# Nine products on ones at the start, a last store in two halves, and twelve of the 44 weight sums made by DMA moved from attention into gate and up

## The chip, the cores and the metric

One core of a Trainium2 chip runs the whole program; the other cores do nothing. The metric is the time of one execution in device microseconds (us). The kernel before took 2303.65 us in the median of three runs (2301.34 to 2307.2). Lower is better. All durations, waits and start times below come from one further execution, the profiled one.

## The reference, cut to what matters

One decoder block on 512 tokens with model width 2048 and a feed-forward width of 5632, everything in fp32:

```python
h = rms_norm(x, g_mix)
# one projection h @ w_in, split into NSA queries/keys/values, gates, and GLA queries/keys/values
x = x + concat(rms_norm(o_nsa), o_gla) @ w_out
hq, hm = rms_norm(x, g_cross), rms_norm(mem, g_mem)         # 256 memory tokens
ck = rms_norm((hm @ w_ck).reshape(B, M, 4, 128), g_ck)       # the "key projection" below
x = x + softmax(cq @ ck.T) @ (hm @ w_cv) @ w_co
hf = rms_norm(x, g_ffn)
gg, uu = split(hf @ w_gu)                                    # gate and up
return x + (silu(gg) * uu) @ w_down                          # down
```

## The kernel before, in words

**Products.** A product of two fp32 operands is made of three products of split operands. `split` (L155 to L160) has ACT cast a tile to its rounded part (`wh`, `qh`, `X`) and DVE subtract to get the rest (`wl`, `ql`); `mm3` then has PE multiply high by high, low by high and high by low. Nearly every product has a 128x128 stationary part and 512 columns. PE is recorded at L98, ACT and DVE mostly at L158 to L160. In the names, `X` is the split input x, `wh`/`wl` a split weight of attention, mixing or cross attention, `qh`/`ql` a split weight of gate, up or down, `PA`/`PB` and `hT`, `ss`, `C`, `T` work tiles, `mm`, `t`, `s`, `o` the pairs of PSUM banks.

**Stages.** The first projection reads x row by row (`load_x`, L334: load, split, square for the norm) and its weights `w_v` (natural order, 0 to about 60 us). Attention (NSA and GLA together) runs to about 640 us, with small pieces of work from generators interleaved by a counter of ticks (`Flows`, L100). Mixing (`w_out`) runs to about 785 us, then the key projection (`project_keys`: four `w_ck` tiles of 2048 columns, each loaded in two pieces of 512 KB by SP at L188 through a pool of two raw tiles named `w`), then the rest of cross attention to about 1010 us. Gate and up take 1010 to 1871 us in eleven blocks n = 0 to 10, each of a phase 1 (loads of 768 KB, L1264, 24 products for each of 8 steps kp) and a phase 2 (loads of 512 KB, L1275, 18 products for each kp). Down runs from 1871 us to the end.

**Sums of weights.** The products of down and of gate and up are made by a scheme with fewer products that needs sums of blocks of weights. Those of `w_down` are made by DMA alone, DRAM to DRAM: a copy of 512 KB from `w_down` into a tile `td` (L145), and a second transfer that adds another block to it (L143, an accumulating transfer). There are 44 such sums for `td`, 88 transfers, and 8 more for tiles `tw` (L1405 and L1409). All of these transfers are issued by POOL, one after the other in its queue, with whatever else POOL issues (spills of attention, loads of `mem_t`, `w_cq`, x1 and h).

**What sets their places.** `SUMS` (L47) is a table of (first tick, last tick, number of sums); the 88 transfers of `td` become marks of `flows`. When a mark is recorded, the copy or the accumulation is issued with a dependency on the PE product recorded last (`last_mm`), so it cannot leave before PE has come there. With this table, 16 sums lie at 92 to 270 us, 4 at 321 to 380, 14 at 440 to 622, and 10 at 690 to 835, that is beside mixing and the key projection. Each `tw` pair (copy and accumulation together) hangs on kp 5 of phase 2 of n = 1 to 8. The dictionary `extra` that `phase` takes names what is to be called after which kp.

**The start.** POOL sets `ones`; ACT casts it to `ones_r` in two halves (L224). The square of every x row is made by ACT directly behind that row's cast (L341), and DVE adds it to `ss` (L343).

**The end.** `gather` (L1584) adds the last product bank to the residual `PA` on DVE and calls `store` (L1579), which issues a 256 KB transfer on SP (L1582).

Of the kernel before, what the change touches and what calls it, by code (L numbers as in the profile page):

```python
# [13 lines left out]
AF = mybir.ActivationFunctionType  # L14
OP = mybir.AluOpType
# [11 lines left out]
AHEAD = 150  # L27
# [16 lines left out]

LAG = 3

SUMS = ((80, 190, 16), (222, 268, 4), (298, 388, 14), (440, 546, 10))  # L47

SV = {}
_n = 0  # L50
# [9 lines left out]
def hybrid_block(ctx: ExitStack, tc: tile.TileContext, x_t, mem_t, sv, cmat, umask, w_a, w_r67, w_v, w_vg, w_v3,  # L60
                 w_vsw, w_gk2, w_c1, w_c2, w_out, w_cq, w_ck, w_cv, w_co, w_gu, w_down, y_t):
    nc = tc.nc
# [24 lines left out]
    def bank(tag):  # L87
        return psp.tile([128, 512], F32, name=tag, tag=tag, bufs={"mm": 3, "s": 2, "t": 2, "o": 1}[tag])
# [3 lines left out]
    def row(tag, dt=F32):  # L92
        return sb([128, 512], tag, BUFS[tag], dt)
# [3 lines left out]
    def mm(*args, **kw):  # L97
        last_mm[0] = PE.matmul(*args, **kw)  # L98
# [56 lines left out]
    def split(hi, lo, src, gain=None):  # L155

        if gain is None:
            return S.copy(hi, src), V.tensor_sub(lo, src, hi)  # L158
        return (S.activation(hi, src, AF.Copy, scale=gain),
                V.scalar_tensor_tensor(lo, src, gain, hi, op0=OP.mult, op1=OP.subtract))  # L160

    def split_row(src, gain=None, tag="X"):
        pair = row(tag, F32R), row(tag, F32R)
        split(*pair, src, gain)
        return pair

    class Weights:
# [53 lines left out]
    ones = pool.tile([128, 64], F32, name="ones")  # L221
    G.memset(ones, 1.0)
    for a in (0, 64):
        S.copy(ones_r[:, a:a + 64], ones)  # L224

    gains = held_vecs[:, NSV:NSV + 2]
    V.tensor_scalar(gains[:, 0:1], vec("g_q"), -HEAD_SCALE, None, op0=OP.mult)
# [103 lines left out]
    xg = []  # L331
    ss = row("ss")

    def load_x(kt):  # L334
        xr = row("st")
        with tc.high_priority(offset=0 if kt < 4 else 40 if kt < 8 else 100):
            nc.sync.dma_start(xr, x_t[:, kt, :])
        xg.append(split_row(xr, vec("g_mix", kt)))
        sq = ss if kt == 0 else row("n")
        with tc.high_priority(offset=200 if kt == KT - 1 else -20 if kt < 4 else 0):  # L340
            S.activation(sq, xr, AF.Square)  # L341
            if kt:
                V.tensor_add(ss, ss, sq)  # L343

    def x_ahead(kq):
        while kq and len(xg) < min(4 * kq + 4, KT):
# [532 lines left out]
    ss = row("ss")  # L879
# [382 lines left out]
    def weights_1(n, kp):  # L1262
        raw = sb1("raw")
        nc.sync.dma_start(raw[:, :1536], w_gu[n, kp, :, 512:2048])  # L1264
        V.tensor_sub(raw[:, 0:1024], raw[:, 0:1024], raw[:, 512:1536])  # L1265
        a = split_cols(raw, 0, 1024)
        V.tensor_add(raw[:, 1536:2048], raw[:, 0:512], raw[:, 1024:1536])
        kept[kp] = sb1("T2")
        S.copy(kept[kp], raw[:, 1536:2048])
        b = split_cols(raw, 1024, 1024)  # L1270
        return part(b, 512, 512), part(b, 0, 512), part(a, 0, 512), part(a, 512, 512)
# [127 lines left out]

    tw = {(step, kp): dram.tile([128, 1024], F32, name="tw", tag="tw", bufs=8) for kp in range(4) for step in (1, 3)}  # L1400

    def make_sum(step, kp):
        def go():
            a, b = (w_down[0, kp], w_down[1, kp]) if step == 1 else (w_down[2, kp], td[kp][:, 1024:])
            i = G.dma_start(tw[step, kp], a)  # L1405
            tc.add_manual_dep(i.ins, last_mm[0].ins.name,
                              mybir.DependencyInfo(mybir.DependencyClass.Sync, mybir.DependencyReason.DATA),
                              reason="in its turn")
            G.dma_start(tw[step, kp], b, accum_op=OP.add, max_dma_last_dim=2048)  # L1409
        return go  # L1410

    ready_made = [make_sum(*k) for k in tw]
    rc2 = []
    gate = []
    hs = None
# [1 line left out]
    for n in range(NB):  # L1417
        if n == 0:
            b1, bp = first_banks
            u, c11 = [sb2("C") for _ in range(2)], [sb2("C") for _ in range(2)]  # L1420
            with tc.high_priority(offset=2 * EVICT):
                for i in range(2):
                    fa = S.copy(u[i], b1[i])
                for i in range(2):
                    fv = V.tensor_add(c11[i], u[i], bp[i])
            bu, b2, b3 = [bank("mm"), bank("mm")], [bank("mm"), bank("o")], [bank("t"), bank("t")]

            def last_sums():
                with tc.high_priority(offset=AHEAD):
                    for kp in (KP - 2, KP - 1):  # L1430
                        with tc.issue_after(splits_b[kp - KP + 3][0].ins), tc.issue_after(splits_b[kp - KP + 3][1].ins):
                            form_sums(kp)

            phase(lambda kp: weights_b(n, kp), (bu, b2, b3), (4, 5, 3), (1, 2, 0), (0, 1, 2), True, 40,
                  {2: [last_sums]}, (fa, fv))
        else:
            b1 = c11 = [bank("mm"), bank("mm")]
            bu = [bank("s"), bank("s")]
            b2 = [bank("t"), bank("t")]
            b3 = [bank("mm"), bank("o")]  # L1440
            phase(lambda kp: weights_1(n, kp), (bu, b1, b2, b3), PHASE_1, (2, 3, 1, 0), (1, 0, 2, 3), True, AHEAD, {},
                  fence)
            u = [sb2("C") for _ in range(2)]
        c22 = [sb2("C") for _ in range(2)]
        with tc.high_priority(offset=EVICT):
            for i in range(2):
                if n:
                    fa = S.copy(u[i], b1[i])
                V.tensor_add(u[i], u[i], bu[i])
            for i in range(2):  # L1450
                V.tensor_add(c22[i], u[i], b2[i])
            for i in range(2):
                fv = V.tensor_add(c22[i], c22[i], b3[i])
        extra = {}
        if hs:
            extra = {2: [turn(hs, n - 1, 0)], 4: [turn(hs, n - 1, 1)], 6: [lambda: gate.append(last_mm[0])]}
            if ready_made:
                extra[5] = [ready_made.pop(0)]
        if n == 0:
            def scales():  # L1460
                ss2 = sb2("C")
                G.dma_start(ss2, ssd)
                rc2.append(token_norm_col(ss, D, NT, ss2))

            phase(lambda kp: weights_c(n, kp), (b2, b3), (2, 6), (0, 1), (0, 1), False, AHEAD, {3: [scales]}, (fv,))
            rc2 = rc2[0]
        else:
            phase(lambda kp: weights_2(n, kp), (b1, b2, b3), PHASE_2, (1, 0, 2), (0, 1, 2), False, AHEAD, extra,
                  (fa, fv))
        g1, g2 = [sb2("C") for _ in range(2)], [sb2("C") for _ in range(2)]  # L1470
        with tc.high_priority(offset=EVICT):
            for i in range(2):
                fa = S.activation(g1[i], c11[i], AF.Silu, scale=rc2[:, i:i + 1])
            for i in range(2):
                V.tensor_add(g2[i], u[i], b2[i])
            for i in range(2):
                fv = V.tensor_add(u[i], u[i], b3[i])
        fence = fa, fv
        for i in range(2):
            S.activation(g2[i], g2[i], AF.Silu, scale=rc2[:, 2 + i:3 + i])  # L1480
        for i in range(2):
            V.scalar_tensor_tensor(g1[i], u[i], rc2[:, i:i + 1], g1[i], op0=OP.mult, op1=OP.mult)
        for i in range(2):
            V.scalar_tensor_tensor(g2[i], c22[i], rc2[:, 2 + i:3 + i], g2[i], op0=OP.mult, op1=OP.mult)
        hs = g1 + g2
# [95 lines left out]
        c = 1024 * b + 512 * j  # L1581
        nc.sync.dma_start(y_t[2 * a + i, :, c:c + 512], res[a, b][x])  # L1582

    def gather(op, a, b, src, x, last=False):  # L1584
        op(res[a, b][x], res[a, b][x], src[x])
        if last:
            store(x, a, b)
# [12 lines left out]
    for step, plan in enumerate(STEPS):  # L1600
# [9 lines left out]
        for kp in range(NK):  # L1610
            if step or kp % 2 == 0:
                load_w(step, kp)
                late_splits(step, kp)

            if kp in (1, NK - 1):
                for r in rs_ if kp == 1 or step == 2 else reversed(rs_):
                    for x in range(4):
                        for k in (kp - 1, kp):
                            down_product(step, r, k, (x,))
                        if step == 3 and kp == NK - 1:  # L1620
                            gather(ADD, *((0, 0), (1, 0))[r], banks[r], x, True)
            elif 1 < kp < NK - 2:
                for r in rs_:
                    down_product(step, r, kp, range(4))
            if step == 0 and kp % 2 and 5 <= kp < 21:
                for m in (kp - 5, kp - 4):
                    if m % 4 == 0:
                        raw = sb1("raw")
                        nc.sync.dma_start(raw, x2d[m // 4])
                    turn_x2(m, raw)  # L1630
            if step == 0 and kp in (2, 4):
                turn(hs, NB - 1, kp // 2 - 1, "t")()
            if step == 0 and kp in (5, 11):
                load_h(0, len(GRP) - (2 if kp == 5 else 1))
            if step < 3 and kp % 4 == 3:
                load_h(step + 1, kp // 4)
# [138 lines left out]
```

## Time and profile before

| what | value |
|---|---|
| median of three runs | 2303.65 us (2301.34 to 2307.2) |
| the profiled execution's own time | 2308.06 us |
| its span, first to last instruction | 2306.3 us |
| mean granted TensorE clock | 0.997 |
| PE busy | 2284.3 us (99%) |
| DVE, ACT, POOL busy | 1662.3 (72%), 1181.8 (51%), 164.0 us (7%) |
| products and transposes on PE | 10764 records |

The profiled execution lies 4.4 us above the median of the runs, and 1.76 us of its own time lie outside the span. Engines are PE (matmul), DVE (vector), ACT (scalar), POOL and SP (here, issuers of transfers). A row of the timeline gives start, duration, engine, line, operation, written tile, read tiles; in brackets stands how long the engine had been idle before it and what it was released by. In rows of the chain of waits stand start, duration, and engine or transfer. The chain of waits leads back from the last instruction, at each step to what released it.

### The profile page before, as it was taken

To read this page: it belongs to the slowest core of one execution; us is meant where nothing else is said; L and a number is where in the kernel's file an instruction comes from. 1 tells how busy PE (TensorE), PEld (TensorE's weight loads), DVE (VectorE), ACT (ScalarE), POOL (GpSimd) and SP (SyncE) were. 2 spreads that over 40 slices of the span, in tenths; PEclk is the share of its full clock that TensorE was granted. 3 is DMA by queue.
4 is the path that set the end of the run, shared out by engine and by line. 5 is a ranking of instruction groups with operands and counts; after the bars stand their busy time and mean duration, and the time that the engine had idled before them with its cause. 6 is when DMAs were issued, how large, how long until landed. Compare 5 with 4: busy or idle time off the path is not lost.

```text
span 2306.3 us, 29509 instructions
## 1 busy us (share of the span) xinstructions
PE 2284.3 (99%) x10764; PEld 1895.6 (82%) x10764; DVE 1662.3 (72%) x2552; ACT 1181.8 (51%) x1857; POOL 164.0 (7%) x240
## 2 busy tenths in 40 slices
PE   8999999999999999999999999999999999999999
PEld 7988888888878878777888888888888888888887
DVE  6478766677775446688888788888887875775685
ACT  6334545556774335665555545544554555444452
POOL 0011100011111100110000000000000000000000
PEclk9999999999999999999999999999999999999999
DMA  6587656466658754685456545644564497766754
GB/s 191 135 195 180 172 155 172 123 174 174 167 170 236 205 161 141 205 219 179 148 180 196 161 140 183 200 155 156 187 189 149 141 333 292 269 230 245 267 207 146
DMA packets 140449, 434.17 MB, mean 188 GB/s; under 512 B 14448, under 2 KB 34928, under 8 KB 136848
## 3 DMA queue, kind: packets, MB, share of 16 engines
q1 hardware_dynamic: 80752, 306.96, 39.5%
q0 software_dynamic: 33824, 96.75, 17.6%
q10 hardware_dynamic: 25728, 28.58, 3.5%
q8 instruction: 84, 1.38, 0.2%
q14 instruction: 61, 0.50, 0.1%
HBM read 390.81 MB, written 94.11 MB: 210 GB/s over the span
## 4 chain that ended last, share of the span: by engine, by line
PE 92%; DVE 3%; DMA 3%; issue 1%; ACT 1%; SPq 0%; ACTq 0%; DVEq 0%
PE mm L98 50%; PE t L98 16%; PE s L98 14%; PE o L98 10%; DVE ql L158 1%; PE t L800 1%; PE s L1361 1%; DVE wl L158 1%; DMA w<-w_ck 1%; DMA raw<-w_down 0%; DMA raw<-w_gu 0%; DMA w<-w_c 0%; ACT wh L158 0%; PE t L1575 0%; DVE PB L158 0%
## 5 line engine op out<-in xcount | busy, mean ns | idle before, releaser
L158 ACT CAST qh<-raw 128x1024 fp32r<-128x1024 f32 (+1 forms) x526 | 510.1, 980 | 480.0 <-PE t L98 126.8
L158 DVE TENSOR_TENSOR ql<-raw,qh 128x1024 fp32r<-128x1024 f32 (+1 forms) x526 | 590.2, 1130 | 149.9 <-PE mm L98 53.2
L98 PE MATMUL mm<-X,wh 128*128 128x512 f32 x1600 | 504.6, 395 | 0.0
L98 PEld LDWEIGHTS mm<-X,wh 128*128 128x128 f32 x1600 | 294.5, 188 | 56.6 <-issue 0.8
L98 PE MATMUL t<-qh,PB 128*128 128x512 f32 x968 | 335.4, 391 | 0.0
L98 PE MATMUL mm<-X,wl 128*128 128x512 f32 x800 | 313.9, 393 | 0.3 <-DVE wl L158 0.3
L98 PE MATMUL mm<-qh,PB 128*128 128x512 f32 x868 | 310.7, 391 | 1.7 <-ACT qh L158 1.7
L158 DVE TENSOR_TENSOR wl<-w,wh 128x1024 fp32r<-128x1024 f32 (+2 forms) x150 | 179.4, 1199 | 163.9 <-ACT wh L158 161.9
L158 ACT CAST wh<-w 128x1024 fp32r<-128x1024 f32 (+2 forms) x150 | 154.2, 1030 | 246.1 <-PE mm L98 169.5
L98 PE MATMUL s<-qh,PB 128*128 128x512 f32 x672 | 232.9, 391 | 0.1
L98 PE MATMUL mm<-qh,PA 128*128 128x512 f32 x640 | 221.7, 389 | 0.0
L98 PEld LDWEIGHTS t<-qh,PB 128*128 128x128 f32 x968 | 181.9, 188 | 37.3
L98 PEld LDWEIGHTS mm<-qh,PB 128*128 128x128 f32 x868 | 163.1, 188 | 36.7 <-ACT qh L158 2.9
L98 PE MATMUL t<-ql,PB 128*128 128x512 f32 x484 | 188.3, 389 | 0.0
L98 PE MATMUL o<-qh,PB 128*128 128x512 f32 x484 | 187.6, 390 | 0.0
L98 PEld LDWEIGHTS mm<-X,wl 128*128 128x128 f32 x800 | 150.4, 188 | 32.8 <-DVE wl L158 1.6
L98 PE MATMUL mm<-ql,PB 128*128 128x512 f32 x434 | 169.8, 391 | 2.1 <-DVE ql L158 2.1
L98 PEld LDWEIGHTS s<-qh,PB 128*128 128x128 f32 x672 | 125.9, 188 | 26.5 <-ACT qh L158 1.0
L98 PEld LDWEIGHTS mm<-qh,PA 128*128 128x128 f32 x640 | 120.1, 188 | 25.3
L98 PE MATMUL s<-ql,PB 128*128 128x512 f32 x336 | 131.5, 391 | 0.2
L98 PE MATMUL mm<-ql,PA 128*128 128x512 f32 x320 | 124.5, 389 | 0.0
L1265 DVE TENSOR_TENSOR raw<-raw 128x1024 f32<-128x1024 f32 x80 | 97.3, 1217 | 31.9 <-DMA raw<-w_gu 31.9
(498 smaller groups left out, 3449.0 us busy)
## 6 DMA issues: line engine op xcount, KB each, us to landing
raw<-w_gu SPq DMA_DIRECT2D x88, 768.0 KB, 4.3
raw<-w_gu SPq DMA_DIRECT2D x88, 512.0 KB, 3.5
raw<-w_down SPq DMA_DIRECT2D x84, 512.0 KB, 4.7
td<-w_down POOLq DMA_DIRECT2D x66, 512.0 KB, 6.6
w<-w_a SPq DMA_DIRECT2D x60, 512.0 KB, 4.5
raw<-td SPq DMA_DIRECT2D x22, 1024.0 KB, 4.9
PB<-h POOLq DMA_DIRECT2D x35, 512.0 KB, 5.7
h<-T ACTq DMA_DIRECT2D x66, 256.0 KB, 4.2
```

The costliest lines, as they stand in the source:

```text
L98: last_mm[0] = PE.matmul(*args, **kw)
L158: return S.copy(hi, src), V.tensor_sub(lo, src, hi)
L800: PE.transpose(tp[:, 128 * (i - j):128 * (i - j) + 128], ps_[b][:, POFF[i] + 128 * j:POFF[i] + 128 * j + 128], ident)
L1265: V.tensor_sub(raw[:, 0:1024], raw[:, 0:1024], raw[:, 512:1536])
L1361: PE.transpose(ps[f][:, 128 * i:128 * i + 128], hs[i][:, c:c + 128], ident)
```

## The change

It makes four edits.

1. Nine products of `ones_r` with itself go into a `t` bank at the very start; nobody reads the bank. `ones_r` is cast by DVE instead of ACT.
2. The square of x row 0 (`ss`) is issued only behind the cast of x row 1.
3. The last store is halved: the last tile of down is added in two parts of 256 columns, the first stored by SP, the second by ACT's queue.
4. `SUMS` keeps 2 sums at ticks 298 to 311 and 10 at 323 to 388 where it had 14 at 298 to 388, and the 10 at ticks 440 to 546 are gone. The remaining 12 sums (24 transfers, `LATE_SUMS`) join the 16 transfers of `tw` in one list of 40; `two_sums` takes two from its head for each of the 20 phases of n = 1 to 10, one after kp 3 and one after kp 7. Copy and accumulation are thus issued apart, each with its own dependency on the last product.

```diff
-SUMS = ((80, 190, 16), (222, 268, 4), (298, 388, 14), (440, 546, 10))
+SUMS = ((80, 190, 16), (222, 268, 4), (298, 311, 2), (323, 388, 10))
+LATE_SUMS = 12
...
-        split(*pair, src, gain)
+        last_cast[0] = split(*pair, src, gain)[0]
...
-        S.copy(ones_r[:, a:a + 64], ones)
+        V.tensor_copy(ones_r[:, a:a + 64], ones)
+    idle = bank("t")
+    for i in range(9):
+        mm(idle.rearrange("p (a n) -> p a n", a=4), ones_r, ones_r[:, None, :].to_broadcast([128, 4, 128]),
+           start=True, stop=True)
...
         xg.append(split_row(xr, vec("g_mix", kt)))
-        sq = ss if kt == 0 else row("n")
+        if kt == 0:
+            first_x.append(xr)
+            return
+        if kt == 1:
+            with tc.high_priority(offset=-20), tc.issue_after(last_cast[0].ins):
+                S.activation(ss, first_x[0], AF.Square)
+        sq = row("n")
         with tc.high_priority(offset=200 if kt == KT - 1 else -20 if kt < 4 else 0):
             S.activation(sq, xr, AF.Square)
-            if kt:
-                V.tensor_add(ss, ss, sq)
+            V.tensor_add(ss, ss, sq)
...
-    def make_sum(step, kp):
+    def make_sum(step, kp, accumulate):
         def go():
-            a, b = (w_down[0, kp], w_down[1, kp]) if step == 1 else (w_down[2, kp], td[kp][:, 1024:])
-            i = G.dma_start(tw[step, kp], a)
+            src = ((w_down[0, kp], w_down[1, kp]) if step == 1 else (w_down[2, kp], td[kp][:, 1024:]))[accumulate]
+            if accumulate:
+                i = G.dma_start(tw[step, kp], src, accum_op=OP.add, max_dma_last_dim=2048)
+            else:
+                i = G.dma_start(tw[step, kp], src)
             tc.add_manual_dep(i.ins, last_mm[0].ins.name,
...
-            G.dma_start(tw[step, kp], b, accum_op=OP.add, max_dma_last_dim=2048)
...
-    ready_made = [make_sum(*k) for k in tw]
+    assert len(sums) == 2 * LATE_SUMS
+    ready_made = sums + [make_sum(*k, accumulate) for k in tw for accumulate in range(2)]
+
+    def two_sums():
+        return {kp: [ready_made.pop(0)] for kp in (3, 7) if ready_made}
...
-            phase(lambda kp: weights_1(n, kp), (bu, b1, b2, b3), PHASE_1, (2, 3, 1, 0), (1, 0, 2, 3), True, AHEAD, {},
+            phase(lambda kp: weights_1(n, kp), (bu, b1, b2, b3), PHASE_1, (2, 3, 1, 0), (1, 0, 2, 3), True, AHEAD, two_sums(),
                   fence)
...
-            if ready_made:
-                extra[5] = [ready_made.pop(0)]
+            extra.update(two_sums())
...
+        if halves:
+            i, j = quad[x]
+            for c, queue in ((0, nc.sync), (256, nc.scalar)):
+                op(res[a, b][x][:, c:c + 256], res[a, b][x][:, c:c + 256], src[x][:, c:c + 256])
+                n = 1024 * b + 512 * j + c
+                queue.dma_start(y_t[2 * a + i, :, n:n + 256], res[a, b][x][:, c:c + 256])
+            return
...
-                            gather(ADD, *((0, 0), (1, 0))[r], banks[r], x, True)
+                            gather(ADD, *((0, 0), (1, 0))[r], banks[r], x, True, (r, x) == (0, 3))
```

PE's first products before, from the first instruction of the kernel on (`X` is x split, `wh` and `wl` the weights of the first projection; the engine, then the shape written):

```order
1 L98 MATMUL mm<-wh,X 128x512
2 L98 MATMUL mm<-wl,X 128x512
3 L98 MATMUL mm<-wh,X 128x512 x2
4 L98 MATMUL mm<-wl,X 128x512
5 L98 MATMUL mm<-wh,X 128x512
6 L98 MATMUL o<-wh,X 128x512
7 L98 MATMUL o<-wl,X 128x512
8 L98 MATMUL o<-wh,X 128x512
9 L98 MATMUL mm<-wh,X 128x512
10 L98 MATMUL mm<-wl,X 128x512
```

And in the changed kernel, where one line is added ahead, so that line numbers are one or more higher:

```order
1 L99 MATMUL t<-ones_r 128x512 x9
2 L99 MATMUL mm<-wh,X 128x512 x2
3 L99 MATMUL o<-wh,X 128x512
4 L99 MATMUL mm<-wh,X 128x512
5 L99 MATMUL mm<-wl,X 128x512
6 L99 MATMUL mm<-wh,X 128x512
7 L99 MATMUL mm<-wl,X 128x512
8 L99 MATMUL mm<-wh,X 128x512
9 L99 MATMUL o<-wl,X 128x512
10 L99 MATMUL o<-wh,X 128x512
```

The nine products stand in front, and of the first twelve real ones the four that need only the high parts come first.

POOL's queue before, at the end of mixing and through the key projection: the last of the ten late sums (`td`), then loads of `w_cq` and `mem_t` for the next projections:

```order
142 L145 DMA td_91<-w_down 128x1024
143 L143 DMA td_91<-td_91 128x2x512
144 L145 DMA td_92<-w_down 128x1024
145 L143 DMA td_92<-td_92 128x2x512
146 L145 DMA td_93<-w_down 128x1024
147 L143 DMA td_93<-td_93 128x2x512
148 L1090 DMA raw_8146<-w_cq 128x1024
149 L1090 DMA raw_8157<-w_cq 128x1024
```

The same place now, from the `mem_t` loads that stood ahead of the ten sums:

```order
122 L900 DMA st_8489<-mem_t 128x512
123 L900 DMA st_8559<-mem_t 128x512
124 L1104 DMA raw_8132<-w_cq 128x1024
125 L1104 DMA raw_8143<-w_cq 128x1024
126 L1104 DMA raw_8132<-w_cq 128x1024
127 L1104 DMA raw_8143<-w_cq 128x1024
```

No sum stands between them any more; the `w_cq` loads follow the `mem_t` loads directly.

POOL's queue now at the end of gate and up, where the last sums (`tw`) meet the first loads of h for down (`PB`):

```order
198 L1531 DMA PB_16125<-h_8850 128x1024
199 L1531 DMA PB_16131<-h_8851 128x1024
200 L1422 DMA tw_9394<-w_down 16x8192
201 L1531 DMA PB_16137<-h_8852 128x1024
202 L1420 DMA tw_9394<-td_75 128x2x512
203 L1531 DMA PB_16143<-h_8853 128x1024
204 L1531 DMA PB_16243<-h_8850 128x1024
205 L1531 DMA PB_16245<-h_8850 128x1024
```

Before, the six loads of h stood there together, with the last `tw` accumulation two blocks (n) ahead of them. On ACT and DVE, besides the start and the end, one addition (L1267 before) and one copy (L1269) stand up to three rows later in each phase of gate and up from its kp 4 on.

More of the change, by code (lines that the diff above doesn't have):

```diff
@@ L160, in split @@
                 V.scalar_tensor_tensor(lo, src, gain, hi, op0=OP.mult, op1=OP.subtract))
+    last_cast = [None]
     def split_row(src, gain=None, tag="X"):
         pair = row(tag, F32R), row(tag, F32R)
-        split(*pair, src, gain)
+        last_cast[0] = split(*pair, src, gain)[0]
         return pair
@@ L332, in hybrid_block @@
     ss = row("ss")
+    first_x = []
     def load_x(kt):
@@ L1582, in store, with gather @@
         nc.sync.dma_start(y_t[2 * a + i, :, c:c + 512], res[a, b][x])
-    def gather(op, a, b, src, x, last=False):
+    def gather(op, a, b, src, x, last=False, halves=False):
+        if halves:
[5 more added lines that the diff above has]
+            return
         op(res[a, b][x], res[a, b][x], src[x])
```

## Prediction

> **What bounds the kernel now.** I read the page first, then the stretches, then the chain of waits and the timeline where a stretch has idle time on PE.
>
> ```profile
> PE 2284.3 (99%) x10764; PEld 1895.6 (82%) x10764; DVE 1662.3 (72%) x2552; ACT 1181.8 (51%) x1857; POOL 164.0 (7%) x240
> ...
> PE 92%; DVE 3%; DMA 3%; issue 1%; ACT 1%; SPq 0%; ACTq 0%; DVEq 0%
> ```
>
> PE is busy for 99% of the span and carries 92% of the chain. The change removes no product that anybody needs, so it can only win where PE idles or runs at a lower clock: at most 22 us of idle (2306.3 − 2284.3), plus lost clock. The stretches (PE, weight loads, DVE, ACT, POOL, then clock, DMA share, GB/s) show where that is:
>
> ```profile
> 690.00:770.00 80.00, 80.00 (x353) 65.85 (x352) 39.82 (x55) 32.01 (x47) 9.85 (x12) 1.00 0.81 230
> ...
> 790.00:830.00 40.00, 37.70 (x157) 30.29 (x156) 17.14 (x25) 16.11 (x34) 3.92 (x5) 0.91 0.73 208
> ...
> 1212.00:1900.00 688.00, 687.75 (x3117) 569.53 (x3116) 555.26 (x686) 348.96 (x450) 15.83 (x23) 1.00 0.56 182
> ```
>
> Mixing (690 to 770 us), where most of the ten removed sums lie, has no idle PE and full clock, although the DMA engines are 81% busy: taking sums away there gains nothing. The key projection (790 to 830 us) idles 2.3 us and has a mean clock of 0.91. Gate and up idle 0.25 us in 688: nothing to win there, only to lose.
>
> **Edit 4, first half: the sums that leave the key projection.** The chain of waits there, and the rows that name its transfers:
>
> ```profile
> 793.58 4.61 DMA w<-w_ck
> ...
> 800.62 7.32 DMA w<-w_ck
> ...
> 808.03 1.05 ACT wh L158
> ...
> 809.11 1.24 DVE wl L158
> ```
>
> ```profile
> DMA to landing us min/median/max: 3.2/4.3/7.3
> ```
>
> ```profile
> 798.38 1.15 POOL L143 DMA_DIRECT2D td<-td  x1 [6.33 <-PE t L98]
> ...
> 807.20 0.39 PE L98 MATMUL t<-wh,e 128*128 128x512 f32 x1
> 809.13 0.50 PE L98 MATMUL t<-wh,on 128*128 128x512 f32 x1 [1.54 <-ACT wh L158]
> 810.39 0.80 PE L98 MATMUL t<-wl,on 128*128 128x512 f32 x1 [0.76 <-DVE wl L158]
> ```
>
> The two raw tiles make a loop: load, cast, subtract, and the next load into the freed tile. The last load (issued at 800.62) took 7.32 us, where the `w_ck` loads together have a median of 4.3 and a minimum of 3.2 (the row of that tile). An accumulating sum had been issued at 798.38, 2.2 us ahead of it. The cast came at 808.03 and PE, dry after its product at 807.20, started at 809.13 and again at 810.39.
>
> The pace of PE: nine products in 2.04 us, 0.227 each, at full clock; three in 1.28, 0.427 each, before the clock rises. The nine between took 0.31 more than 2.04, so it rose at about 11.2:
>
> ```profile
> 9.36 1.28 PE o L98 x3
> 10.64 2.35 PE mm L98 x9
> ...
> 13.68 2.04 PE mm L98 x9
> ```
>
> So the gaps cost (809.13 − 807.20 − 0.227) + (810.39 − 809.13 − 0.227) = 1.70 + 1.03 = 2.7 us. To close both, the subtraction, which ended at 810.35, must end by 807.66, when the second product would follow in pace: the load must be 2.7 us shorter, 4.6 instead of 7.32. The median of 4.3 does that even with the load before it (4.61) unchanged; without sums both should be nearer 3.7 and leave two us more. I take the whole 2.7. Against it: stores of x and `w_out` loads share this time and stay. The `w_cq` loads that stood behind the sums in POOL's queue do not move in here: they wait for a buffer that DVE frees at 873.
>
> ```profile
> 873.10 2.21 POOL L1090 DMA_DIRECT2D raw<-w_cq  x4 [38.31 <-DVE X L160]
> ```
>
> The clock: 0.91 over 40 us is a loss of 3.6 us of full speed, some 0.3 of it in PE's idle time, so 3.3 us. It stands directly behind the gaps, and no stretch quoted without gaps has it. I take it to go with them. The Trainium skill (TensorE: Matmul & The Clock Gate, Why this matters for your kernels) has a rule against that: no idle gaps above about 3 us between bursts, since one window of idle brings the lower clock. The two gaps here are 1.5 and 0.8 us of idle and yet the clock fell; by the page's rule they would not be its cause, and edit 4 would gain 2.7 here and not 6.0.
>
> How much of the 3.3 is in ordinary runs is unknown: the profiled execution (2308.06) is 4.4 us above the median of the runs, and those spread by 5.9. I put half of it, 1.6, against the median.
>
> **Edits 1 and 2: the start.** The chain of waits up to the first product; then, of the timeline, the setting of `ones` and the cast of x row 1:
>
> ```profile
> 1.18 3.06 DMA st<-x_t
> ...
> 4.33 0.72 ACT X L159
> 5.05 0.52 ACT ss L341
> 5.57 0.52 ACT wh L158
> ...
> 6.13 3.23 PE mm L98 x6
> ```
>
> ```profile
> 0.73 0.15 POOL L222 MEMSET ones<- 128x64 f32 x1 [0.29 <-POOLq L1767]
> ...
> 8.73 0.72 ACT L159 ACTIVATE X<-st,vecs 128x512 fp32r<-128x512 f32 x1 [1.45 <-DMA st<-x_t]
> ```
>
> Without the square (0.52) the first cast of weights, and the first product, come at about 5.6. Nine products on ones at 0.427 take 3.8 us and start once DVE has cast `ones` (set at 0.88), at some 1.3 by estimate: they end at 5.1, ahead of the first real product, so they cost nothing. The clock rose after 5.1 us of work (6.13 to 11.2); counted from 1.3 it would rise near 6.4. The first twelve products then end near 8.7 instead of 11.4. But the second k tile needs x row 1, whose cast starts at 8.73 when its load lands; with the DVE part behind it, the low half is there at 10.2. Its twelve products can end at about 12.5, against 14.1 before: 1.6 us, not the 2.6 that the clock alone gives. I take 1.4, since the norm of x at 42 us hangs on the last x load and not on PE:
>
> ```profile
> 41.77 0.69 DVE L158 TENSOR_TENSOR n<-ss,n 128x512 fp32r<-128x512 f32 x1
> ```
>
> ```profile
> 42.76 0.62 PE L98 MATMUL s<-n,ones_r 128*128 128x512 f32 x2
> ```
>
> The subtraction ends at 42.46 and PE reads at 42.76: 0.3 us of slack. The loads ahead are paced by buffers that the splits free, so most of them move with the start; if the last did not, 0.3 of the 1.6 would be left. Bounds: 0.3 to 2.6. If the cover of the nine products were gone (x and weights there at once) they would cost up to 3.8 us; they are not.
>
> **Edit 3: the end.**
>
> ```profile
> 2302.07 0.69 DVE L1585 TENSOR_TENSOR PA<-PA,t 128x512 f32<-128x512 f32 x1 [0.67 <-PE t L98]
> ```
>
> Behind this row (its end 2302.76) lie 3.5 us to the end of the span: one 256 KB store. Half the addition saves at most 0.3 for the first half; the second ends as late as before, its transfer is half as long and goes by another queue. Bounds: 0 and 0.5; I take 0.3.
>
> **Edit 4, second half: the sums that enter gate and up.** Forty transfers, one after kp 3 and one after kp 7 in each of 20 phases; 16 of them are there already. POOL waits for nothing else that is urgent there, but the bandwidth is shared:
>
> ```profile
> raw<-w_gu SPq DMA_DIRECT2D x88, 768.0 KB, 4.3
> ```
>
> ```profile
> DMA to landing us min/median/max: 3.8/5.7/12.3
> ```
>
> The second row is the tile `tw`: a sum's transfer may be in flight for up to 12.3 us. The stage's tightest place is the start of each phase 1. Here in one of the ten turns are the loads' first issue, the pair of `tw`, and ACT and PE:
>
> ```profile
> 1387.81 36.39 SPq L1264 DMA_DIRECT2D raw<-w_gu  x8
> ```
>
> ```profile
> 1394.30 0.51 POOL L1405 DMA_DIRECT2D tw<-w_down  x1 [72.29 <-PE o L98]
> 1398.57 1.18 POOL L1409 DMA_DIRECT2D tw<-td  x1 [3.77 <-DMA tw<-w_down]
> ```
>
> ```profile
> 1398.54 0.61 ACT L1269 COPY T<-raw 128x512 f32<-128x512 f32 x1
> 1400.44 1.05 ACT L158 CAST qh<-raw 128x1024 fp32r<-128x1024 f32 x1 [1.29 <-PE t L98]
> 1401.40 1.26 ACT L1473 ACTIVATE C<-mm,rc 128x512 f32<-128x512 f32 x2
> 1402.55 1.05 ACT L158 CAST qh<-raw 128x1024 fp32r<-128x1024 f32 x1
> ...
> 1403.13 1.24 PE L98 MATMUL s<-qh,PB 128*128 128x512 f32 x3
> ```
>
> The last cast ends at 1403.60, just as PE takes it (third product of the last row). It looks as if any delay shows. But ACT had waited 1.29 us for PE to free a buffer, not for a load: the first two loads may land 1.3 us later and nothing changes. A kp of phase 2 has 18 products, 4.1 us. The copy after kp 3, two kp ahead of 1394.30, thus leaves at 1386.1, 1.7 us ahead of the first of these loads, and overlaps it by some 2 us; shared evenly, the load lands 1 us later. Covered. The accumulation after kp 7 leaves at 1402.5 for 1398.57, against loads that are not the tight ones. I take +0.3 for the whole; the bounds are −0.3 (all idle gone) and +17 (below).
>
> At the end of up, loads of h (`PB`) now stand behind the last `tw` accumulation, which waits for the phase's last product:
>
> ```profile
> 1867.72 2.17 POOL L1511 DMA_DIRECT2D PB<-h  x4 [21.68 <-DMA h<-T]
> ```
>
> ```profile
> 1885.19 1.05 ACT L158 CAST PB<-PB 128x1024 fp32r<-128x1024 f32 x1 [0.54 <-ACT T L1365]
> ```
>
> Some now leave 4 to 5 us later than these four did. The first of their casts came 17.5 us after the first issue, and it was not a load that it waited for; 5 us less leaves 12. I take 0, at most 2.
>
> **The sum.** Against the profiled execution: −1.4 − 2.7 − 3.3 − 0.3 + 0.3 = −7.4, so 2300.7. Against the median of the runs, with half of the clock: 2303.65 − 1.4 − 2.7 − 1.6 − 0.3 + 0.3 = 2297.95, **2298.0 us**.
>
> **Rivals.**
>
> *The clock's dip stays* (0.15). It may have another cause than the gaps. The gaps go, the 3.3 stays: 2303.65 − 4.1 = 2299.6. For it: the idle times are short. Against it: the dip starts within 3 us of them and nowhere without idle.
>
> *The gaps stay, or the change does nothing there* (0.08). The loop of two raw tiles is slow without any sum (4.61 us for a load that one met only at its end), so PE still runs dry. Left are the start and the end: 2303.65 − 1.4 = 2302.3. Against it: 4.6 suffices.
>
> *The whole dip was in the ordinary runs too, and the start gives its upper bound* (0.20): 2303.65 − 2.6 − 2.7 − 3.3 − 0.5 = 2294.6.
>
> *Slower: the copy after kp 3 of phase 2 takes the bandwidth from the first load of phase 1* (0.10). If the load is 2.2 us later, a whole overlap, less the 1.3 of cover, 0.9 shows on PE at each of ten turns: +9, and 2297.95 − 0.3 + 9 = 2306.7; if it is as late as the long `w_ck` load (7.32 − 4.3 = 3.0), it is +17 and 2314.7. It decides from a delay of 1.3 us. For it: loads beside a sum lasted 7.32 at the key projection. The Trainium skill (DMA: Bandwidth & Descriptors, Queues, rings and completion order) says that each DMA engine takes packets from its queues in turn, so a copy holds back a load from another queue; this trace agrees, with the 7.32. Against it: eight turns carried a pair already, and 688 us of the stage hold 0.25 us of idle.
>
> **Chances.** The forecast has the remaining 0.47. A measurement of this kernel can tell about 0.3%, 6.9 us, from no change: faster lies below 2296.7, slower above 2310.6. The forecast's own spread is 2294.5 to 2301 and has under half below 2296.7 (0.21); the case with the whole dip adds 0.16: faster 0.37. Slower is the last rival at its upper prices: 0.07. The rest, 0.56, is within. The range runs from 2293.5 (the third rival with 1 us of spread between runs) to 2304.0 (the second with 1.7).
>
> **What would show it.** The stretch 790 to 830 (some 2 us earlier) should have under 0.5 us of idle and clock 1.00, the longest `w_ck` load be under 4.6 us; with the clock at 0.91 and no idle, the first rival is right. The first real product should be at 5.6 at the pace of 0.227, and the thirteenth behind x row 1's cast. Idle time on PE above 2 us in gate and up, at the third cast of phase 1, makes me wrong to the slow side. Wrong to the fast side: idle time removed that I have not named.

## The result and the profile after

The changed kernel took 2332.24 us in the median (2331.43 to 2333.97), the kernel before 2304.54 beside it: a ratio of 1.0116, 95% interval 1.0104 to 1.0129. It is slower by 28 us where 6 us faster was forecast, far above the range. The profiled execution took 2332.38 us with a span of 2330.4, against 2308.06 and 2306.3 before, so the two traces hold 24.1 us of the difference.

The chain by engine on the page of the changed kernel:

```profile
PE 82%; DVE 7%; DMA 6%; issue 3%; ACT 1%; ACTq 0%; SPq 0%; DVEq 0%; POOL 0%; POOLq 0%
```

PE carried 92% of it before. Nine of the ten points that it lost went to DVE, to transfers and to issue. The same three stretches as before (PE, weight loads, DVE, ACT, POOL, clock, DMA share, GB/s), now of the changed kernel:

```profile
690.00:770.00 80.00, 80.00 (x355) 66.27 (x354) 39.36 (x53) 31.56 (x47) 0.00 (x0) 1.00 0.45 153
790.00:830.00 40.00, 40.00 (x182) 33.12 (x181) 18.06 (x22) 16.68 (x33) 0.00 (x0) 1.00 0.48 156
1212.00:1900.00 688.00, 673.49 (x3005) 548.87 (x3004) 539.33 (x665) 338.71 (x428) 30.97 (x40) 1.00 0.61 186
```

The key projection is clean: no idle time, clock 1.00 for 0.91. Gate and up, where PE idled 0.25 us in 688, idle 14.5. What PE waited for from 1090 to 1900 us (total, times, longest); before, this answer has no row at all:

```profile
PE s L99 <- ACT qh L159: 9.6, 9, 1.1
PE t L99 <- DVE ql L159: 4.5, 8, 1.0
PE s L99 <- DVE ql L159: 1.5, 9, 0.2
```

The first and the third row have nine waits each, one in each turn from a phase 2 to the next phase 1; of the eight in the second row seven lie in turns and one in the last phase 2. To see how much each stage gained or lost, I laid the starts of the same product in both traces side by side:

| product of the kernel before at | its place | changed kernel earlier (−) or later (+), us |
|---|---|---|
| 59.94 | first projection | −1.99 |
| 780.09 | ahead of the key projection | −1.53 |
| 829.99 | behind it | −7.29 |
| 1130.10 | first block of gate and up with sums | −6.52 |
| 1809.91 | after nine turns | +17.60 |
| 1874.97 | after the last phase 2 (n = 10) | +18.86 |
| 1945.00 | first step of down | +24.31 |
| 2289.97 | last step of down | +24.33 |

So the start gained 2.0, the key projection 5.8; nine turns lost 24.1, 2.7 each, the last phase 2 lost 1.3, and the start of down 5.5.

One turn, in the changed kernel. The chain of waits, from the last load of phase 2 on:

```profile
1141.36 4.02 DMA raw<-w_gu
...
1146.01 0.70 DVE ql L159
1146.71 0.02 issue
1146.73 6.52 DMA raw<-w_gu
...
1153.34 1.22 DVE raw L1279
1154.56 0.34 DVE T L1381
...
1155.95 0.68 DVE raw L1281
1156.64 0.34 DVE T L1382
1156.97 0.33 DVE T L1383
1157.31 1.14 DVE raw L1279
...
1166.97 1.20 PE s L99 x4
```

The first load of phase 1, issued at 1146.73, took 6.52 us. Ahead of it stands the copy of a sum on POOL, recorded after kp 3:

```profile
1144.21 0.56 POOL L146 DMA_DIRECT2D td<-w_down  x1 [16.00 <-PE o L99]
```

It landed at 1150.10 by the trace, so 3.4 us lie beside the load; before, the same load took 4.09. Over the nine turns this load took 4.0 to 4.3 us before and 5.7 to 6.8 in the changed kernel. From the load's landing to PE's wait the chain is DVE, one instruction behind the other, with short times of issue between.

### The profile page after: what moved, and what is told of

It reads as the page before. It is cut to its first block, busy times and chain, and to the rows that moved or that the text cites. A ratio compares the mean times of both kernels' runs of the same rounds, so it can differ in the third digit from the quotient of the medians.

```text
span 2330.4 us, 29549 instructions
## 1 busy us (share of the span) xinstructions
PE 2295.3 (98%) x10773; PEld 1895.6 (81%) x10773; DVE 1662.1 (71%) x2555; ACT 1184.9 (51%) x1855; POOL 163.9 (7%) x240
## 4 chain that ended last, share of the span: by engine, by line
PE 82%; DVE 7%; DMA 6%; issue 3%; ACT 1%; ACTq 0%; SPq 0%; DVEq 0%; POOL 0%; POOLq 0%
PE mm L99 46%; PE t L99 14%; PE s L99 13%; PE o L99 8%; DMA raw<-w_gu 4%; DVE ql L159 3%; DMA raw<-w_down 1%; DVE raw L1279 1%; PE t L814 1%; ACT qh L159 1%; DVE raw L1281 0%; DVE C L1495 0%; DVE wl L159 0%; DMA PB<-h 0%; DMA w<-w_vsw 0%
```

## Experiments

All times are medians in us beside the kernel before on the same chip.

| kernel | time | before | ratio (95% interval) |
|---|---|---|---|
| changed kernel | 2332.24 | 2304.54 | 1.0116 (1.0104 to 1.0129) |
| start_end | 2301.65 | 2303.79 | 0.9984 (0.9975 to 0.9994) |
| all_in_1 | 2298.31 | 2303.79 | 0.9974 (0.9964 to 0.9984) |
| copy_kp5 | 2308.38 | 2303.79 | 1.0018 (1.0009 to 1.0027) |
| copy_kp2 | 2326.90 | 2303.79 | 1.0101 (1.0084 to 1.0118) |
| accs_in_2 | 2304.08 | 2303.92 | 1.0000 (0.9990 to 1.0009) |
| copies_in_2 | 2329.13 | 2303.92 | 1.0112 (1.0097 to 1.0127) |
| h_by_pool | 2328.49 | 2303.92 | 1.0116 (1.0100 to 1.0132) |
| end_acc | 2304.70 | 2303.92 | 1.0000 (0.9991 to 1.0010) |
| load_more | 2313.49 | 2305.91 | 1.0029 (1.0019 to 1.0039) |
| acc_in_down | 2301.68 | 2305.91 | 0.9982 (0.9973 to 0.9992) |
| all_in_1_again | 2301.15 | 2305.91 | 0.9978 (0.9968 to 0.9988) |

My theory: the copy after kp 3 of phase 2 makes the loads around the turn late, and these have no slack; and the last accumulation holds up the start of down. The rivals: any 24 more transfers in the stage cost that much; the accumulations do it; or the new order at the start does. In the following, a product's place against the kernel before is read as in the table above.

### start_end: edits 1 to 3 alone

```diff
-SUMS = ((80, 190, 16), (222, 268, 4), (298, 311, 2), (323, 388, 10))
-LATE_SUMS = 12
+SUMS = ((80, 190, 16), (222, 268, 4), (298, 388, 14), (440, 546, 10))
+LATE_SUMS = 0
...
-            phase(... True, AHEAD, two_sums(),
+            phase(... True, AHEAD, {},
...
-            extra.update(two_sums())
+            if ready_made:
+                extra[5] = [ready_made.pop(0), ready_made.pop(0)]
```

> Edits 1 to 3 alone; the 44 sums lie where they lay before. The first part of my theory is that the start gained 2.0 us and the end 0.2 in the changed kernel, and that everything lost is edit 4: this run should stand 2.2 us under the kernel before, near 2302.3, with gate and up at 78 us a block. The rival, that the reordered start or another order of instructions on ACT and DVE costs something in gate and up, expects more than 2310.

It stood 2.1 us under before, as expected; its products are 2.3 us ahead at 60 us, and in nine turns nothing is lost (−2.1 at 1130, −3.6 at 1810). All that is lost is edit 4. Its key projection, the stretch 790 to 830, still has the gaps and the lower clock:

```profile
790.00:830.00 40.00, 37.42 (x156) 30.13 (x155) 16.62 (x21) 14.72 (x31) 3.38 (x4) 0.91 0.71 204
```

### all_in_1, and all_in_1_again: all forty transfers in phase 1

```diff
-            phase(... True, AHEAD, two_sums(),
+            phase(... True, AHEAD, two_sums((2, 3, 5, 6)),
...
-            extra.update(two_sums())
```

> The changed kernel with all forty transfers in the ten phases 1 (after kp 2, 3, 5 and 6) and none in phase 2. My theory: the copy after kp 3 of phase 2 makes the first two loads of phase 1 late by 2.4 us, and the last pair crowds the start of down. Both are gone here, so it stands near 2300 (2299 to 2302): 25.3 for ten turns and 5.6 at the start of down come off 2332.2, and what the key projection and the start gained stays. The rival, that the stage is full and any 24 more transfers cost about 1 us each wherever they lie in it, expects some 2330 still.

> The same kernel as all_in_1, beside the two others on one chip: 2297 to 2299.5, and faster than before by 0.2 to 0.35%.

It gave 2298.31, inside what was expected, and 0.9974 of before; again, 0.9978, but 2301.15, above the absolute time that I gave, since before itself was 2 us slower on that chip. The stretch of gate and up with the same 40 transfers:

```profile
1212.00:1900.00 688.00, 688.00 (x3131) 571.23 (x3130) 557.91 (x683) 358.49 (x468) 31.87 (x43) 1.00 0.62 199
```

No idle time at a DMA share of 0.62, as high as the changed kernel's 0.61. So the stage is not full; the place decides. This version beats both kernels, with an interval below 1 in both series. Against start_end on the same chip, moving the sums from the key projection into phase 1 is worth 3.3 us in ordinary runs (2301.65 − 2298.31).

### copy_kp5 and copy_kp2: another place for the copy of phase 2

```diff
-            extra.update(two_sums())
+            for kp, gos in two_sums((5, 7)).items():
+                extra[kp] = extra.get(kp, []) + gos
```

and the same with (2, 7).

> The changed kernel with the copy of phase 2 after kp 5 instead of kp 3, where the pairs of the kernel before had theirs; the accumulation stays after kp 7, phase 1 as changed. My theory (the copy's place): the turns are free again, 22 to 25 us come off, and only the start of down (up to 5.6) stays lost: 2305 to 2309. The rival (the accumulation after kp 7, or the number of transfers): 2325 or more.

> The changed kernel with the copy of phase 2 after kp 2, 4.1 us earlier than in the changed kernel. My theory: it lands before or just as the first load of phase 1 is issued, so at least 15 of the 25 us of the turns come off: 2305 to 2317, the start of down still lost. The rival, that the sums delay something of phase 2 itself, or that the accumulation does it, expects 2325 or more.

copy_kp5's time came as expected, though its turns were not quite free: nine lost 5.0 (−9.77 to −4.80) instead of 24.1, the start of down 3.9. copy_kp2's did not, it lies in the rival's range: nine turns lost 19.9 (−6.31 to +13.58), only 5 us of the time came back, although the copy (1139.45 to 1143.23) had landed 5 us ahead of the first load of phase 1. Its chain of waits shows why:

```profile
1132.95 5.25 DMA raw<-w_gu
...
1138.90 1.05 DVE ql L159
...
1141.35 5.86 DMA raw<-w_gu
...
1147.84 0.70 DVE ql L159
1148.56 4.21 DMA raw<-w_gu
...
1152.87 1.23 DVE raw L1279
```

The loads of phase 2 and of the next phase 1 hang together: each takes a raw tile that DVE frees after the subtraction of an earlier one. The copy lengthened the last load of phase 2 (5.86 us; in all_in_1 4.00), and the first of phase 1, itself at 4.21, left later by as much. My theory was too narrow: not the first load alone is tight, but the string of loads ahead of the turn, and the rival was right that the copy delays a load of phase 2.

### accs_in_2 and copies_in_2: only accumulations, or only copies, in phase 2

```diff
-... True, AHEAD, two_sums(),
+... True, AHEAD, two_sums((3, 5, 7)),
...
-            extra.update(two_sums())
+            for kp, gos in two_sums((7,)).items():
+                extra[kp] = extra.get(kp, []) + gos
```

and for the copies two_sums((3,)) in phase 2, with four transfers in the first phase 1.

> The changed kernel with phase 1 taking copy, accumulation and copy (after kp 3, 5 and 7) and phase 2 only the second accumulation, after kp 7, where it is in the changed kernel. My theory, that the copy after kp 3 alone holds up the turns: turns free, the start of down still 4 to 5.5 us late: 2302 to 2305. The rival, that the accumulations after kp 7 of phase 2 share in the loss of the turns: over 2312.

> The counterpart: phase 2 of n = 1 to 9 takes only a copy, after kp 3 as in the changed kernel, and phase 1 all else; the list is used up ahead of the last phase 2. My theory: nine turns lose 2.5 us each, the start of down loses nothing: 2298.3 + 22 to 24, so 2320 to 2323. The rival (the accumulations do it): under 2308.

With the accumulations nine turns lost 0.1 us (−8.38 to −8.25) and the start of down 4.6. With the copies nine turns lost 27.1 (−9.41 to +17.65), 3.0 each and more than the 22 to 24 that I gave, and the start of down 0.4. The copies after kp 3 are the turns' whole loss; the accumulations after kp 7 have no part in it.

### h_by_pool: the stores of h from POOL's queue

```diff
-            S.dma_start(d[:, 0, c:c + 256], e[:, x])
+            G.dma_start(d[:, 0, c:c + 256], e[:, x])
             for p, t in ((1, o), (3, a), (5, b)):
-                S.dma_start(d[:, p:p + 2, c:c + 256], t.rearrange("q (p c) -> q p c", p=2))
+                G.dma_start(d[:, p:p + 2, c:c + 256], t.rearrange("q (p c) -> q p c", p=2))
```

> The changed kernel with the stores of h issued by POOL instead of ACT. My theory of why the 1.3 us that ACT waited in the turn were no slack: ACT stood at its own store of h, which waits for a DVE addition that stands behind the loads' sums. Without the store in ACT's queue the casts of a turn come up to 1.3 us earlier beside the late load, so of the 2.5 lost per turn 0.5 to 1.3 come back: 2319 to 2327. The rival, that ACT waited there for PE to free a buffer, as the bracket in the timeline has it: no change, 2330 to 2334.

On ACT, in the turn:

```profile
1156.03 0.62 ACT L1283 COPY T<-raw 128x512 f32<-128x512 f32 x1 [1.62 <-DVE raw L1281]
1156.56 1.04 ACT L159 CAST qh<-raw 128x1024 fp32r<-128x1024 f32 x1
```

The cast now follows the copy at once. That fits the store, but does not prove it, since the copy itself now came late, behind DVE. What settles it is ACT's own queue in the kernel before, where a store stands between the copy at 1398.54 and the cast at 1400.44:

```profile
1399.98 0.37 ACTq L1375 DMA_DIRECT2D h<-T  x1
```

It leaves as DVE's addition ends (start 1399.53, 0.42 us), and the cast follows it. In all nine turns of the kernel before the cast starts 0.49 to 0.50 us behind the end of that addition, while the last signal of PE came anywhere from 0 to 0.4 us ahead of the cast. So the 1.29 us that ACT waited there, put down to PE by the bracket, were the store at the head of its queue.

But the turns got nothing back (nine lost 25.1, −10.79 to +14.29); the time, 2328.49, lies between the two ranges, and what it is lower by was there ahead of the turns. The store was not what set the turn either: ACT's copy now waited 1.62 us for DVE. The stores moved, some DVE work stands in another order and the loads at that place lasted longer in some turns (up to 9.5 us), so this run does not say what one store costs.

### load_more: a longer first load, with no sum near

```diff
+        if kp == 0:
+            nc.sync.dma_start(raw[:, 1536:2048], w_gu[n, kp, :, 0:512])
         nc.sync.dma_start(raw[:, :1536], w_gu[n, kp, :, 512:2048])
```

on top of all_in_1; what it loads more is overwritten.

> All forty transfers in phase 1 (2298.3), and ahead of the first load of each phase 1 a load of 256 KB more by SP into a part of the same raw tile that is overwritten later: the first load lands later with no sum near it. What it measures is the slack of that load. My theory: DVE works without a break from the landing of that load to the cast that PE waits for, so there is no slack, and each of ten turns loses what the landing is late by, 0.6 to 1.2 us: 2304 to 2310. The rival, that the 1.3 us of ACT's waiting in the turn are slack of the load: 2298 to 2299.5.

Nine turns lost 9.2 us (−1.80 to +7.41) where all_in_1_again lost none (−4.98 to −6.63): 1.0 each, with no sum near the load. DVE waits for that load in the turn, and for its landing alone:

```profile
1158.47 1.23 DVE L1281 TENSOR_TENSOR raw<-raw 128x1024 f32<-128x1024 f32 x1 [4.00 <-DMA raw<-w_gu]
```

The total, 2313.49, is above the 2304 to 2310 expected: 5 us were lost between 1000 and 1130. Of these, 2.3 lie at the turn from n = 0 to n = 1, which has the longer load too and where all_in_1_again loses nothing; the rest lies in the first block, where all_in_1_again also loses 1.6.

The theory of no slack is nearly right. The table takes the landing of the first load of phase 1, counted against PE's products and compared with the kernel before, and what a turn lost; both are means over the nine turns, in us:

| kernel | the load landed later by | a turn lost |
|---|---|---|
| accs_in_2 | 0.0 | 0.0 |
| copy_kp5 | 0.9 | 0.6 |
| load_more | 1.4 | 1.0 |
| copy_kp2 | 2.5 | 2.2 |
| changed kernel | 3.0 | 2.7 |
| h_by_pool | 3.1 | 2.8 |
| copies_in_2 | 3.3 | 3.0 |

Whatever made the load late, the copy of a sum beside it, a copy ahead of it or a longer load, the turn lost all but 0.3 us of it. So the slack is about 0.3 us, and not 1.3.

### end_acc and acc_in_down: the last accumulation

end_acc is all_in_1 with the last transfer after kp 7 of the last phase 2; acc_in_down has it in down instead:

```diff
+            if step == 0 and kp == 9:
+                ready_made.pop(0)()
```

> All forty transfers in phase 1, but for the very last accumulation, which stands after kp 7 of the last phase 2 as in the changed kernel. My theory of the start of down: this one transfer puts four loads of h 4 us back in POOL's queue and shares the bandwidth with the first loads of w_down, and costs 4 to 5.5 us alone: 2302.3 to 2304. The rival, that the start of down was late because of the turns before it: 2298.3 as without.

> All forty transfers in phase 1 but for the last accumulation, which is now put behind kp 9 of the first step of down, in POOL's queue behind the loads of h that it held up in the run where it stood after kp 7 of the last phase 2 (2304.7). My theory: what cost 6 us there was that it waits for PE at the head of the queue, and shares the bandwidth at the start of down; here it does neither, and little is lost: 2298 to 2300.5. The rival, that an accumulation anywhere in the crowded first step of down costs its bandwidth: 2302 or more.

The start of down lost 7.1 us with it in its place (−8.53 to −1.42), more than the 4 to 5.5 expected, and 0.4 with it in down (−7.73 to −7.34). In medians end_acc is level with before; acc_in_down is above the 2298 to 2300.5 expected, but only 0.5 us above its neighbour all_in_1_again. POOL's rows of end_acc, then of acc_in_down:

```profile
1859.19 0.53 POOL L1532 DMA_DIRECT2D PB<-h  x1 [21.68 <-DMA h<-T]
1863.27 1.23 POOL L1420 DMA_DIRECT2D tw<-td  x1 [3.56 <-PE o L99]
1864.03 2.12 POOL L1532 DMA_DIRECT2D PB<-h  x3
```

```profile
1860.00 2.14 POOL L1530 DMA_DIRECT2D PB<-h  x4 [21.69 <-DMA h<-T]
```

In the first, the accumulation stands at the head of the queue until PE is through kp 7, 3.56 us, and three loads of h behind it leave 4 us later; in the second the four leave together. The two runs do not tell the wait from the shared bandwidth, since the later place removes both.

## Why the prediction was wrong

- **Start, −1.4.** Right: −2.0 in the changed kernel (−1.2 to −2.6 over all twelve traces). The first product came at 6.02 and not 5.6, since its weights were still in flight. The first two products still took about 0.5 us each; the pace of 0.23 came at about 7.4.

```profile
1.65 3.67 DMA P<-w_v
...
6.02 1.22 PE mm L99 x2
```

- **Key projection, −2.7 and −3.3.** Right: −5.8 in the traces. The dip of the clock went with the gaps: both profiles with gaps there (before 1.54 and 0.76 us, start_end 1.83 and 0.75) have 0.91, and the changed kernel and all_in_1, without gaps, 1.00. By the rule of the Trainium skill (TensorE: Matmul & The Clock Gate, Why this matters for your kernels), idle gaps of 1.5 and 0.8 us are too short for that; the measurement decides. The half that I counted for ordinary runs made 4.3 us; start_end and all_in_1 differ by 3.3.
- **End, −0.3.** Right: the lag fell by 0.2 from 2290 to the end.
- **Loads of h, 0.** Wrong by 5.5 us. I had the delay (4 to 5 us) but measured its cover by the first cast of h, at 1885, and by the loads of h alone. The chain of waits goes through the loads of `w_down` beside them: in the changed kernel one lasted 10.57 us, where it had taken 6.39 before, and ACT's cast and copies and then PE's transposes stand behind it:

```profile
1898.18 10.57 DMA raw<-w_down
1908.82 1.05 ACT qh L159
1909.87 0.48 ACT T L1378
```

- **Gate and up, +0.3.** This is the step that failed, by 25 us. It read: ACT "had waited 1.29 us for PE to free a buffer, not for a load: the first two loads may land 1.3 us later and nothing changes". Both halves were wrong. The wait was ACT's own store of h, as its row under h_by_pool shows; the bracket names PE, whose signal merely came last ahead of the cast. And the slack had to be looked for on the engine that the load feeds. These are DVE's rows of the kernel before in the same turn:

```profile
1392.17 1.22 DVE L1265 TENSOR_TENSOR raw<-raw 128x1024 f32<-128x1024 f32 x1 [2.57 <-DMA raw<-w_gu]
1393.31 0.42 DVE L1367 TENSOR_TENSOR T<-T,T 128x256 f32<-128x256 f32 x1
1393.65 1.22 DVE L158 TENSOR_TENSOR ql<-raw,qh 128x1024 fp32r<-128x1024 f32 x1
...
1399.53 0.42 DVE L1370 TENSOR_TENSOR T<-T,T 128x256 f32<-128x256 f32 x1
```

DVE had waited 2.57 us for the first load, and from its landing on no row has idle time ahead of it, up to the addition at 1399.53 that the store, and with it the cast at 1400.44, waited for. A load that lands later moves all of that; by the table under load_more its slack is 0.3 us. Beside this the delay itself was mis-sized: 1 us taken, 2.4 measured (6.52 for 4.09). The overlap of 2 us behind it goes with a copy of some 3.7 us, about the shortest in the row that the prediction showed (3.8); the copy took 5.89, and 3.4 of it lay beside the load.

The rival on the slow side was the right one in mechanism and place, the copy after kp 3 and the first load of phase 1, with a chance of 0.10. It was priced at +9 for a load 2.2 us late, because it too took off the 1.3 us of cover; without that it would have said +22 in ten turns, and 2320. Its argument against, "eight turns carried a pair already", counted pairs that came two kp later (at 1394.30 in the turn shown), when the first load had landed (1392.1). By the rule of the Trainium skill that it named (DMA: Bandwidth & Descriptors, Queues, rings and completion order), transfers of two queues take turns on the DMA engines; this trace agrees, with 6.52 us beside a copy.

## What to carry to other kernels

A bracket that names what ended an idle time covers compute instructions; where the engine also issues transfers, look for one between the two rows before calling the idle time slack. The slack of a load is read on the engine that it feeds first: if that engine waited for the load and then has no idle time up to the critical work, the slack is close to nothing (0.3 us here), and what makes that load late costs nearly its whole delay in every round. When work is moved to fill a quiet stage, place it by the round's tight point, here in the middle of a phase and not ahead of its end.

## What was not expected of the hardware

A copy of 512 KB from DRAM to DRAM beside a load of 768 KB lengthened the load from 4.09 to 6.52 us and took 5.89 itself, while over the whole stage a DMA share of 0.62 with no idle PE (all_in_1) was possible. The mean share says nothing of the moment. And the granted clock fell to 0.50 at 809.8, 0.7 us behind the end of the gap of 1.54 us and ahead of the end of the second (0.76), and stayed there for 6.8 us; in start_end it did the same from 807.1 on. Such gaps do not always bring it: in copy_kp5 PE waits 2.1 and 0.8 us for ACT at the start of down, and the clock from 1884 to 1900 is 1.00. What decides between the two is open.
